# The S5 layer of a four-layer trunk: inputs regrouped through DRAM, and twelve gated outputs accumulated over K

## The chip, the cores and the metric

The kernel runs on one core of a Trainium2 chip. The metric is the device time of one execution in microseconds. "Before" is the median of three runs. The profile is one more execution, taken with the hardware profiler.

The engines are named as the profile names them. PE is TensorE, the matrix unit; PEld is its loading of weights. DVE is VectorE, ACT is ScalarE, POOL is GpSimd, and SP is SyncE, which here only issues DMAs. A matmul multiplies a weight tile (up to 128 rows by 128 columns, held in the array) with a moving tile and writes a PSUM bank. PSUM has eight banks of 128 x 512 floats here.

## The reference

The model is a trunk of four layers over one sequence of 256 tokens with 1024 channels. Layer i uses mixer i mod 3: forgetting attention (layers 0 and 3), an S5 state-space layer (layer 1), or multi-scale pooling (layer 2). A SwiGLU channel mixer (hidden width 2816) follows each. RMSNorm stands ahead of every part, and the residual is added behind it. This case is about layer 1:

```python
u = (h @ w_in).astype(F32)                                    # 256 x 1024
u_g = u.reshape(B, S, S5_GROUPS, S5_GROUP)                    # 64 groups of 16 channels
lam_bar = jnp.exp(lam * dt)                                   # 64 complex states per group
bu = jnp.einsum('gpc,bsgc->bsgp', b_bar, u_g)
_, states = lax.associative_scan(combine, (lam_seq, bu), axis=1)   # s[t] = lam_bar s[t-1] + bu[t]
y = jnp.einsum('gcp,bsgp->bsgc', c_mat, states).real.reshape(B, S, D_MODEL)
y = y + d.astype(F32) * u
g = jax.nn.gelu(y).astype(h.dtype)
val, gate = jnp.split(g @ w_glu, 2, axis=-1)
return val * jax.nn.sigmoid(gate)
```

Everything is float32. The large products are computed with the weights and the activations split into a high and a low part, three matmuls for each product.

## The kernel before

**Layout and weights.** Activations lie channel-major: eight tiles (index d, k or m) of 128 channels by 256 tokens. The weights are a list of *units* of at most 128 x 1040 floats, in the order of use (`units`, line 56). `unit` (line 102) hands out the next one. It first issues the DMA of the unit three further on (`fetch`, line 81, on SyncE's queue, four buffers `raw`), and then splits the unit two further on into high and low parts (`split_unit`, line 92: line 98 on ScalarE, line 99 on VectorE; five buffers `hl`). `term` (line 159) is the three matmuls of one 128 x 128 weight block, and `dense` (line 164) is one unit of them, 24 matmuls for one output tile. All matmuls are issued at line 157.

**Order.** A tile framework with a planner sets each engine's order of instructions. It starts from program order, simulates the engines, and lets a ready later instruction go ahead where an earlier one isn't ready; it also writes the semaphore waits, and a buffer is reused when its readers are done. On top of that the kernel has a clock of its own. `tick` (line 117) advances it after every six dense matmuls (four where two outputs are computed side by side). `at(n, fn)` files a piece of work n ticks ahead, and such a piece is queued behind the last dense matmul on TensorE. So the small work of S5 is woven into the dense work by due times.

**The S5 stage** (`s5`, line 780). The recurrence is cut into blocks of four tokens. Writing token t as 4j + r, each channel tile m needs 64 steps j of four phases r. A preparation (`prepare`, line 507), which runs during layer 0, computes for each m the tables of this scheme and stores them in DRAM (`s5d`): E, the injection weights of the four phases; tab, cosine, sine and decay per step; CX and KT, the output weights and the direct part. In the stage:

- `tables` (line 833) loads E, tab and par of tile m, on SyncE, at tick 1 + 5m. E and tab have two buffers, par three.
- The dense product with `w_s5` gives u for m = 0 and 1 side by side, then for one m after the other: 12 ticks, then four ticks for each. `evict` (line 788) scales it into u, laid out by phase as 128 channels x 4 phases x 64 steps.
- `core` (line 843), at tick 10 + 5m: for the real and the imaginary part, for each of four phases r and four groups of rows i, one matmul of E's 32 rows with u's 32 rows (line 854), accumulated over r in the PSUM tile e. It takes four banks, of which the pool `p4` holds one copy. Then VectorE rotates by cosine and sine (lines 862 to 865), scans both parts over the 64 steps of four groups (line 867), rotates back (870, 871) and writes the states sx (873, 874).
- `emit` (line 877), six ticks after the core: four full-array matmuls KT x u, 32 matmuls of 32 columns CX x sx, GELU on ScalarE (line 888), and the split into G, the eight tiles of g.
- Gating: g @ `w_glu` has eight pairs of outputs (value and gate). The first two pairs accumulate over k as G[k] appears, in two banks (lines 808 to 818). The other six pairs are dense products of their own, after all of G is there (lines 824 to 826). Each pair ends in a sigmoid, a product and the residual add (828 to 830), and `settled` (line 197) prepares the next FFN's input from it.

PSUM's eight banks are two for "acc", two for "tp" (KT and CX outputs, transposes, norms) and four that serve either as four "P" banks or as e; `open_quad` (line 150) switches between the two.

Of the kernel before, what the change touches and what calls it, by code (L numbers as in the profile page):

```python
# [16 lines left out]
D = 1024  # L17
N = 256
# [12 lines left out]
PREP_RATES = (0.08, 0.33)  # L31


class Trunk:
# [21 lines left out]
    def units(self):  # L56
# [8 lines left out]
        for l in range(self.layers):  # L65
# [6 lines left out]
            elif kind == 1:  # L72
                u.extend(a["w_s5"][m] for m in range(8))
                u.extend(a["w_glu0"][k] for k in range(4))
                u.extend(a["w_glu1"][d] for d in range(12))
            else:
                u.extend((a["w_pool"][:, 0:1024], a["w_pool"][:, 1024:2048]))
# [429 lines left out]
    def prepare(self):  # L507
# [194 lines left out]
        def gains(m):  # L702
            state["gains"] = m
            kp = self.bank("tp")
            for ri in range(2):
                for i in range(4):
                    self.mm(kp[32 * i:32 * i + 32, 0:128], XS[:, ri, 3, i], cxv[:, 0:4, i, ri], ri == 0, ri == 1)
# [6 lines left out]
        def inject(m, ri):  # L714
            pe = pp.tile([128, 4, 128], F32, tag="pe", name="pe", bufs=2)
            tp = self.bank("tp").rearrange("p (t s) -> p t s", t=4)
            for i in range(4):
                nc.tensor.transpose(tp[:, i], XS[:, ri, i].rearrange("p g c -> p (g c)"), self.ident)
# [5 lines left out]
        for m in range(8):  # L724
# [14 lines left out]
            for ri in range(2):  # L739
                for g in range(2):  # L740
                    r, c = slice(64 * g, 64 * g + 64), slice(16 * g, 16 * g + 16)
                    nc.scalar.copy(XS[r, ri, 0:3, :, c], xc[r, ri].rearrange("p (t i c) -> p t i c", t=3, i=4))
                    nc.scalar.copy(XS[r, ri, 3, :, c], bb[r, ri, qs])
# [36 lines left out]
    def s5(self, l):  # L780
# [7 lines left out]
        def evict(m, P):  # L788
            u = mp.tile([128, 4, 64], F32, tag="u", name="u", bufs=4)
            v = lambda z: z.rearrange("p (j r) -> p r j", r=4)  # L790
            nc.vector.tensor_tensor(out=u, in0=v(P), in1=v(self.R), op=ALU.mult)
            self.at(max(1, 10 + 5 * m - self.now + t0), lambda: self.core(m, u, G))

        t0 = self.now
        for m in range(8):
            self.at(1 + 5 * m, lambda m=m: self.tables(m))
        for m in range(0, 8, 2):
            P = [self.bank("acc" if m else "P")[:, 0:N] for _ in range(2)]
            if m == 0:
                self.dense(P, X)  # L800
                self.open_quad()
# [31 lines left out]
    def tables(self, m):  # L833
# [3 lines left out]
        tab = mp.tile([128, 3, 256], F32, tag="tab", name="tab", bufs=2)  # L837
        nc.sync.dma_start(tab.rearrange("p a b -> p (a b)"), self.s5d[m][:, 1024:1792])
# [4 lines left out]
    def core(self, m, u, G):  # L843
# [176 lines left out]
```

## Time and profile before

| | |
|---|---|
| Median of three runs | 1147.97 us (1147.48 to 1149.78) |
| The profiled execution's own time | 1147.19 us |
| Its span, first to last instruction | 1145.4 us |
| TensorE busy | 1117.1 us, 98% of the span |
| VectorE busy | 869.5 us, 76% |
| ScalarE busy | 681.6 us, 60% |
| Mean granted TensorE clock | 0.994 |
| Bytes moved by DMA | 224.98 MB, 196 GB/s on average |
| S5 stage, about | 335 to 444 us |

The rows quoted below come from several views. The *timeline* lists instructions in order of time, merging neighbours of one kind: start, length, engine, line, operation, output <- inputs, shapes, xcount, and in brackets the idle time before them and what ended it. *Groups by form* list line, engine, operation, shapes and count, then total busy us, mean ns of one, and idle time before them. *Stretches* give each engine's busy time within a window. *Waits* list who waited for whom: total us, times, longest. *DMA issues* list output <- input, queue, count, KB of each, and median us from issue to landing. Matmuls are pipelined and their recorded lengths overlap, so the distance between two starts says more than a length. An f32 matmul shows as two records, one of the split products as one.

### The profile page before, as it was taken

What the parts mean: (1) busy time and instruction counts of PE and PEld (TensorE: products, weight loads), DVE (VectorE), ACT (ScalarE), POOL (GpSimd) and SP (SyncE); (2) the same over time, 40 slices, a digit from 0 to 9 for tenths busy, and PEclk for the clock granted to TensorE, in tenths of its full rate; (3) what the DMA queues carried; (4) which work ended last, traced back from release to release, by engine and by line L of the source; (5) the groups of instructions that cost most, each with busy time, mean ns of one, the idle gap of its engine ahead of it and who ended that gap; (6) DMA issues with size and microseconds to landing.
All of it is one profiled execution on the core that took longest, in us unless ns stands there. A gap on an engine that the chain in (4) does not pass through costs nothing. (4 is left out here: it accounts for less than half of the span.)

```text
span 1145.4 us, 22385 instructions
## 1 busy us (share of the span) xinstructions
PE 1117.1 (98%) x8706; PEld 1026.8 (90%) x8706; DVE 869.5 (76%) x1647; ACT 681.6 (60%) x1273; POOL 132.0 (12%) x167
## 2 busy tenths in 40 slices
PE   6999999999999999999999899999999999999996
PEld 6988999999999999888888888888899899888886
DVE  6999976888959975988756688876656767988663
ACT  6467665777763254766554676665545776666551
POOL 1188000111110000000000000000004720000000
PEclk9999999999999999999999899999999999999998
DMA  8655375787888744755666255566666544755661
GB/s 270 222 182 175 122 238 189 245 264 216 264 321 324 275 140 150 234 189 188 181 177 191 93 186 194 191 178 186 196 196 218 162 140 149 214 188 189 181 188 49
DMA packets 63210, 224.98 MB, mean 196 GB/s; under 512 B 7648, under 2 KB 7984, under 8 KB 62976
## 3 DMA queue, kind: packets, MB, share of 16 engines
q1 hardware_dynamic: 56368, 200.86, 54.7%
q0 software_dynamic: 6160, 22.00, 5.8%
q8 instruction: 68, 1.11, 0.4%
q10 hardware_dynamic: 576, 0.69, 0.2%
q14 instruction: 38, 0.31, 0.1%
HBM read 208.81 MB, written 14.71 MB: 195 GB/s over the span
## 5 line engine op out<-in xcount | busy, mean ns | idle before, releaser
L157 PE MATMUL P<-X,hl 128*128 128x256 f32 (+1 forms) x4560 | 678.7, 308 | 1.3 <-ACT y L503 1.3
L157 PEld LDWEIGHTS P<-X,hl 128*128 128x128 f32 x4560 | 616.3, 189 | 52.1 <-issue 8.9
L99 DVE TENSOR_TENSOR hl<-raw,hl 128x1024 fp32r<-128x1024 f32 (+3 forms) x363 | 435.8, 1202 | 137.3 <-ACT hl L98 129.6
L98 ACT CAST hl<-raw 128x1024 fp32r<-128x1024 f32 (+3 forms) x363 | 372.1, 1028 | 174.1 <-PE acc L157 72.6
L157 PE MATMUL acc<-H,hl 128*128 128x512 f32 (+1 forms) x1628 | 251.7, 315 | 0.0
L157 PEld LDWEIGHTS acc<-H,hl 128*128 128x128 f32 x1628 | 226.8, 188 | 21.1 <-issue 0.8
L183 ACT COPY lo<-P 128x256 f32<-128x256 f32 x126 | 46.7, 371 | 102.9 <-PE P L157 102.7
L184 DVE TENSOR_TENSOR t<-P,lo 128x256 f32<-128x256 f32 x126 | 53.3, 424 | 44.6 <-ACT lo L183 44.6
L411 POOL TENSOR_SCALAR nb<-nb,c 128x128 f32<-128x128 f32 (+1 forms) x64 | 67.2, 1063 | 1.1
L157 PE MATMUL acc<-X,hl 128*128 128x256 f32 (+1 forms) x384 | 61.3, 301 | 0.2
L244 POOL TENSOR_TENSOR rs<-rs,mhalf 128x2 f32<-128x2 f32 x9 | 6.5, 719 | 474.8 <-DVE rs L243 474.8
L157 PEld LDWEIGHTS acc<-X,hl 128*128 128x128 f32 x384 | 50.6, 189 | 3.9 <-DVE X L210 0.4
L432 ACT ACTIVATE pt<-pt,st 128x128 f32<-128x128 f32 (+1 forms) x64 | 28.5, 447 | 21.7 <-DVE st L430 21.3
L157 PE MATMUL P<-hl,X 128*128 128x336 f32 (+1 forms) x192 | 41.1, 333 | 0.0
L279 ACT ACTIVATE t<-t 128x256 f32<-128x256 f32 x88 | 36.8, 418 | 6.7 <-DVE t L278 3.7
L209 ACT ACTIVATE X<-x,gains 128x256 fp32r<-128x256 f32 x55 | 27.7, 505 | 15.7 <-DVE x L264 14.9
L218 ACT ACTIVATE s<-x 128x256 f32<-128x256 f32 x63 | 25.6, 406 | 15.9 <-DVE x L264 13.1
L157 PEld LDWEIGHTS P<-hl,X 128*128 128x128 f32 x192 | 33.7, 199 | 0.0
L157 PE MATMUL acc<-hl,X 128*128 128x352 f32 x96 | 25.1, 345 | 8.7 <-DVE X L207 7.5
L210 DVE SCALAR_TENSOR_TENSOR X<-x,gains,X 128x256 fp32r<-128x256 f32 x56 | 26.9, 481 | 5.5 <-ACT X L209 5.5
L278 DVE TENSOR_TENSOR t<-t,R 128x256 f32<-128x256 f32 x66 | 28.0, 424 | 1.8
L281 DVE TENSOR_TENSOR t<-t 128x256 f32<-128x256 f32 x66 | 28.0, 424 | 1.7
(179 smaller groups left out, 855.3 us busy)
## 6 DMA issues: line engine op xcount, KB each, us to landing
raw<-in_w_gu SPq DMA_DIRECT2D x176, 512.0 KB, 3.4
raw<-in_w_dn SPq DMA_DIRECT2D x64, 512.0 KB, 3.6
raw<-in_w_qk SPq DMA_DIRECT2D x32, 512.0 KB, 4.0
raw<-in_w_dn SPq DMA_DIRECT2D x32, 384.0 KB, 3.2
raw<-in_w_fo SPq DMA_DIRECT2D x16, 512.0 KB, 3.6
raw<-in_w_glu SPq DMA_DIRECT2D x16, 512.0 KB, 4.9
raw<-in_w_vf SPq DMA_DIRECT2D x15, 520.0 KB, 4.6
nb<-nd POOLq DMA_DIRECT2D x24, 256.0 KB, 5.6
```

What stands on the lines that cost most here:

```text
L98: nc.scalar.copy(hl[:, 0, s], raw[:, s])
L99: nc.vector.tensor_tensor(out=hl[:, 1, s], in0=raw[:, s], in1=hl[:, 0, s].bitcast(F32), op=ALU.subtract)
L157: return self.nc.tensor.matmul(out, lhsT=lhsT, rhs=rhs, start=start, stop=stop).ins
L183: nc.scalar.copy(lo, o[:, N:])
L184: nc.vector.tensor_tensor(out=t, in0=o[:, 0:N], in1=lo, op=ALU.add)
L209: nc.scalar.activation(self.X[:, d, 0], x, AF.Identity, scale=g)
L210: nc.vector.scalar_tensor_tensor(out=self.X[:, d, 1], in0=x, scalar=g, in1=self.X[:, d, 0].bitcast(F32), op0=ALU.mult, op1=ALU.subtract)
L278: nc.vector.tensor_tensor(out=t, in0=t if wide else G, in1=R, op=ALU.mult)
L279: nc.scalar.activation(t, t, AF.Silu)
L281: nc.vector.tensor_tensor(out=h, in0=h if wide else U, in1=t, op=ALU.mult)
L411: nc.gpsimd.tensor_scalar(out=nb[:, i], in0=nb[:, i], scalar1=self.c[t][:, 4 * n + i:4 * n + i + 1], scalar2=None, op0=ALU.add)
L432: nc.scalar.activation(pt, pt, AF.Exp, bias=st[:, 0:1], scale=-1.0, accum_out=st[:, 1:2])
```

## The change

1. **Injection.** E keeps its size but is ordered so that for each group of rows i its 128 rows are the four phases (4 phases x 32 channels). The preparation's XS is laid out accordingly. The core then needs one matmul of 128 rows for each i and each of the two parts, eight in all, into one "tp" bank.
2. **Regrouping u.** These matmuls want u with phase and channel together on the partitions. `evict` therefore writes u to a DRAM tile `ud` (SyncE), and five ticks later four DMAs (SyncE) read it back as `ue`: 32 partitions for each phase, runs of 64 floats. `emit` still uses u itself, so u has eight buffers instead of four.
3. **Times.** Tables are due at tick 1 + 6m, core m at 18 + 6.3m but at least ten ticks after its `evict`, and `emit` seven ticks after the core.
4. **Gating.** Six pairs (twelve outputs) accumulate over k in six banks (four "P", two "acc"), with `w_glu` regrouped into 16 units of 128 x 768, two for each k. Two pairs stay as dense products, four units of 128 x 1024. The bank switch `open_quad` is no longer called here.
5. **Signed sine.** ScalarE writes a negated copy of the sine row into a fourth row of tab. The pairs of an add and a subtract (864 and 865, 873 and 874) become one 512-wide add each, with the parts read in reversed order.

```diff
             elif kind == 1:
                 u.extend(a["w_s5"][m] for m in range(8))
-                u.extend(a["w_glu0"][k] for k in range(4))
-                u.extend(a["w_glu1"][d] for d in range(12))
+                u.extend(a["w_glu0"][k] for k in range(16))
+                u.extend(a["w_glu1"][d] for d in range(4))
...
-                nc.tensor.transpose(tp[:, i], XS[:, ri, i].rearrange("p g c -> p (g c)"), self.ident)
+                nc.tensor.transpose(tp[:, i], XS[:, ri, i].rearrange("p t c -> p (t c)"), self.ident)
...
-                    nc.scalar.copy(XS[r, ri, 0:3, :, c], xc[r, ri].rearrange("p (t i c) -> p t i c", t=3, i=4))
-                    nc.scalar.copy(XS[r, ri, 3, :, c], bb[r, ri, qs])
+                    nc.scalar.copy(XS[r, ri, :, 0:3, c], xc[r, ri].rearrange("p (t i c) -> p i t c", t=3, i=4))
+                    nc.scalar.copy(XS[r, ri, :, 3, c], bb[r, ri, qs])
...
         def evict(m, P):
-            u = mp.tile([128, 4, 64], F32, tag="u", name="u", bufs=4)
+            u = mp.tile([128, 4, 64], F32, tag="u", name="u", bufs=8)
             v = lambda z: z.rearrange("p (j r) -> p r j", r=4)
             nc.vector.tensor_tensor(out=u, in0=v(P), in1=v(self.R), op=ALU.mult)
-            self.at(max(1, 10 + 5 * m - self.now + t0), lambda: self.core(m, u, G))
+            nc.sync.dma_start(self.ud[m], u.rearrange("p r j -> p (r j)"))
+            ue = mp.tile([128, 4, 64], F32, tag="ue", name="ue", bufs=4)
+
+            def load():
+                for r in range(4):
+                    nc.sync.dma_start(ue[32 * r:32 * r + 32],
+                                      self.ud[m].rearrange("(i c) (r j) -> r c i j", i=4, r=4)[r])
+
+            self.at(5, load)
+            self.at(max(10, FIRST_CORE + 63 * m // 10 - self.now + t0), lambda: self.core(m, u, ue, G))
...
-            self.at(1 + 5 * m, lambda m=m: self.tables(m))
+            self.at(1 + 6 * m, lambda m=m: self.tables(m))
...
-                self.open_quad()
                 evict(0, P[0])
...
-        acc = [self.bank("acc") for _ in range(2)]
+        outs = [self.bank(t) for t in ("P", "P", "P", "P", "acc", "acc")]
         for k in range(8):
             while self.emitted < k + 1:
                 self.tick()
-            if k % 2 == 0:
+            for h in range(2):
                 hl = self.unit()
-            for d in range(2):
-                for h in range(2):
-                    c = (k % 2 * 4 + 2 * d + h) * 128
-                    self.term(acc[d][:, h * N:h * N + N], hl, slice(c, c + 128), G, k, k == 0 and h == 0, k == 7 and h == 1)
-                self.tick()
-        self.open_quad()
+                for d in range(3):
+                    for s in range(2):
+                        c = (2 * d + s) * 128
+                        self.term(outs[3 * h + d][:, s * N:s * N + N], hl, slice(c, c + 128), G, k,
+                                  k == 0 and s == 0, k == 7 and s == 1)
+                    self.tick()
         for d in range(8):
-            if d < 2:
-                V, S = acc[d][:, 0:N], acc[d][:, N:2 * N]
+            if d < 6:
+                V, S = outs[d][:, 0:N], outs[d][:, N:2 * N]
             else:
-                V, S = self.bank("P")[:, 0:N], self.bank("P")[:, 0:N]
+                V, S = [self.bank("tp")[:, 0:N] for _ in range(2)] if d == 6 else [self.bank("P")[:, 0:N] for _ in range(2)]
...
-        e = self.p4.tile([128, 4, 512], F32, tag="e", name="e")
+        nc.scalar.activation(tab[:, 3], tab[:, 1], AF.Identity, scale=-1.0)
+        e = self.bank("tp").rearrange("p (a n) -> p a n", a=2)
         for ri in range(2):
-            for r in range(4):
-                for i in range(4):
-                    rows = slice(32 * i, 32 * i + 32)
-                    self.mm(e[:, i, 64 * ri:64 * ri + 64], E[rows, ri, r], u[rows, r], r == 0, r == 3)
-        two = lambda z: z.unsqueeze(1).broadcast_to([128, 2, 256])
-        c2, s2 = two(tab[:, 0]), two(tab[:, 1])
+            for i in range(4):
+                self.mm(e[:, ri, 64 * i:64 * i + 64], E[:, ri, i], ue[:, i], True, True)
+        c2 = tab[:, 0].unsqueeze(1).broadcast_to([128, 2, 256])
+        sn = tab[:, 1:4:2]
...
-        nc.vector.tensor_tensor(out=ij(A), in0=ev, in1=ij(c2), op=ALU.mult)
-        nc.vector.tensor_tensor(out=ij(B), in0=ev, in1=ij(s2), op=ALU.mult)
-        nc.vector.tensor_tensor(out=A[:, 0], in0=A[:, 0], in1=B[:, 1], op=ALU.add)
-        nc.vector.tensor_tensor(out=A[:, 1], in0=A[:, 1], in1=B[:, 0], op=ALU.subtract)
+        nc.vector.tensor_tensor(out=A, in0=e, in1=c2, op=ALU.mult)
+        nc.vector.tensor_tensor(out=B, in0=e[:, ::-1], in1=sn, op=ALU.mult)
+        nc.vector.tensor_tensor(out=A, in0=A, in1=B, op=ALU.add)
...
-        nc.vector.tensor_tensor(out=B, in0=A, in1=s2, op=ALU.mult)
-        v4 = lambda z: z.rearrange("p (i j) -> p i j", i=4)[:, :, 0:63]
-        nc.vector.tensor_tensor(out=sx[:, 0, :, 1:64], in0=v4(C[:, 0]), in1=v4(B[:, 1]), op=ALU.subtract)
-        nc.vector.tensor_tensor(out=sx[:, 1, :, 1:64], in0=v4(C[:, 1]), in1=v4(B[:, 0]), op=ALU.add)
-        self.at(6, lambda: self.emit(m, u, CX, KT, sx, G))
+        nc.vector.tensor_tensor(out=B, in0=A[:, ::-1], in1=sn[:, ::-1], op=ALU.mult)
+        v4 = lambda z: z.rearrange("p a (i j) -> p a i j", i=4)[:, :, :, 0:63]
+        nc.vector.tensor_tensor(out=sx[:, :, :, 1:64], in0=v4(C), in1=v4(B), op=ALU.add)
+        self.at(7, lambda: self.emit(m, u, CX, KT, sx, G))
```

`FIRST_CORE` is 18. `layout` reorders `w_glu` for the new units.

More of the change, by code (lines that the diff above doesn't have):

```diff
@@ L31 @@
 PREP_RATES = (0.08, 0.33)
+FIRST_CORE = 18
 class Trunk:
@@ L706, in gains @@
                 for i in range(4):
-                    self.mm(kp[32 * i:32 * i + 32, 0:128], XS[:, ri, 3, i], cxv[:, 0:4, i, ri], ri == 0, ri == 1)
+                    self.mm(kp[32 * i:32 * i + 32, 0:128], XS[:, ri, i, 3], cxv[:, 0:4, i, ri], ri == 0, ri == 1)
             for i in range(4):
@@ L836, in tables @@
         nc.sync.dma_start(E.rearrange("p a b c -> p (a b c)"), self.s5d[m][:, 0:1024])
-        tab = mp.tile([128, 3, 256], F32, tag="tab", name="tab", bufs=2)
-        nc.sync.dma_start(tab.rearrange("p a b -> p (a b)"), self.s5d[m][:, 1024:1792])
+        tab = mp.tile([128, 4, 256], F32, tag="tab", name="tab", bufs=2)
+        nc.sync.dma_start(tab[:, 0:3].rearrange("p a b -> p (a b)"), self.s5d[m][:, 1024:1792])
         par = mp.tile([128, 1536], F32, tag="par", name="par", bufs=3)
@@ L841, in tables, with core @@
         self.tabs[m] = (E, tab, par)
-    def core(self, m, u, G):
+    def core(self, m, u, ue, G):
         nc, mp = self.nc, self.mp
@@ L859, in core @@
         C = mp.tile([128, 2, 256], F32, tag="C", name="C", bufs=1)
-        ev = e[:, :, 0:128].rearrange("p i (a j) -> p a i j", a=2)
-        ij = lambda z: z.rearrange("p a (i j) -> p a i j", i=4)
-        nc.vector.tensor_tensor(out=ij(A), in0=ev, in1=ij(c2), op=ALU.mult)
-        nc.vector.tensor_tensor(out=ij(B), in0=ev, in1=ij(s2), op=ALU.mult)
-        nc.vector.tensor_tensor(out=A[:, 0], in0=A[:, 0], in1=B[:, 1], op=ALU.add)
-        nc.vector.tensor_tensor(out=A[:, 1], in0=A[:, 1], in1=B[:, 0], op=ALU.subtract)
+        nc.vector.tensor_tensor(out=A, in0=e, in1=c2, op=ALU.mult)
+        nc.vector.tensor_tensor(out=B, in0=e[:, ::-1], in1=sn, op=ALU.mult)
+        nc.vector.tensor_tensor(out=A, in0=A, in1=B, op=ALU.add)
         for ri in range(2):
@@ L915, in run @@
         self.early = {0: [piece(1, 3)], 1: [piece(3, 8)]}
+        self.ud = [self.dp.tile([128, 256], F32, name=f"ud{m}") for m in range(8)]
         self.s5d = [self.dp.tile([128, 3328], F32, name=f"s5d{m}") for m in range(8)]
@@ L986, in layout @@
     w = f["s5_w_glu"][0].reshape(D, 2, 8, 128)
-    o["w_glu0"] = w[:, :, 0:2].reshape(4, 2, 128, 2, 2, 128).transpose(0, 2, 1, 4, 3, 5).reshape(4, 128, 1024)
-    o["w_glu1"] = np.stack([tiles(w[:, h, 2:].reshape(D, 768)) for h in range(2)], 1).reshape(12, 128, 1024)
+    o["w_glu0"] = w[:, :, 0:6].reshape(8, 128, 2, 2, 3, 128).transpose(0, 3, 1, 4, 2, 5).reshape(16, 128, 768)
+    o["w_glu1"] = np.stack([tiles(w[:, h, 6:].reshape(D, 256)) for h in range(2)], 1).reshape(4, 128, 1024)
     o["w_pool"] = f["pool_w"][0].reshape(4, 2, 128, 256).transpose(2, 0, 1, 3).reshape(128, 2048)
```

## The prediction, made before the result was known

> **What bounds the kernel now.** First I read the head of the page, then the stretches of the S5 stage, then TensorE's timeline in that stage, and last its waits. "Core m" below is the work that the function `core` issues for channel tile m.
>
> ```profile
> span 1145.4 us, 22385 instructions
> PE 1117.1 (98%) x8706; PEld 1026.8 (90%) x8706; DVE 869.5 (76%) x1647; ACT 681.6 (60%) x1273; POOL 132.0 (12%) x167
> ```
> ```profile
> 343.50:400.00 56.50, 55.19 (x1143) 52.18 (x1144) 52.93 (x94) 16.56 (x22) 0.00 (x0) 1.00 0.83 302
> 400.00:410.70 10.70, 10.55 (x190) 9.67 (x189) 6.47 (x12) 4.75 (x7) 0.00 (x0) 1.00 0.31 96
> 410.70:443.80 33.10, 33.10 (x283) 33.10 (x282) 24.99 (x39) 19.68 (x33) 0.00 (x0) 1.00 0.55 175
> ```
> The stretches give start and end, length, then busy time and instructions of PE, PEld, DVE, ACT, POOL, granted clock, DMA share, GB/s. TensorE sets the pace: 55.19 of 56.50 us while the cores run, all of 33.10 us afterwards. VectorE is second and nearly full in the first stretch (52.93 of 56.50), so a change there counts only if it frees TensorE or holds it up. The edit can gain only TensorE time within the stage, and this is how one core looks there:
>
> ```profile
> 394.51 2.77 PE L157 MATMUL acc<-X,hl 128*128 128x256 f32 x22
> 397.21 2.02 PE L157 MATMUL e<-u,E 32*128 32x64 f32 x64
> 399.15 0.98 PE L157 MATMUL acc<-X,hl 128*128 128x256 f32 x6
> 399.97 1.31 PE L157 MATMUL tp<-u,par 128*128 128x256 f32 x8
> 401.21 1.10 PE L157 MATMUL tp<-sx,par 128*32 128x64 f32 x64
> 402.24 3.49 PE L157 MATMUL acc<-X,hl 128*128 128x256 f32 x24
> 405.57 1.31 PE L157 MATMUL tp<-u,par 128*128 128x256 f32 x8
> ```
> ```profile
> 409.09 1.79 PE L157 MATMUL acc<-X,hl 128*128 128x256 f32 x12
> 410.72 33.23 PE L157 MATMUL P<-X,hl 128*128 128x256 f32 x280
> 443.78 0.40 PE L157 MATMUL acc<-X,hl 128*128 128x512 f32 x1
> ```
> Since the durations overlap, I use differences of start times. A dense matmul costs (443.78 - 410.72)/280 = 0.118 us, and a tick of the schedule (six of them) 0.71. The group e took 399.15 - 397.21 = 1.94, and entering it 397.21 - 394.51 - 22 x 0.118 = 0.10 more: **2.04 us per core**. The KT group took 1.24, the sx group 402.24 - 401.21 = 1.03.
>
> **The change, part by part.**
>
> *The e matmuls.* Before: 32 matmuls per core, each of 32 rows, shown as 64 records (an f32 matmul leaves two). After: eight of 128 rows, so 16 records of 128x128 weights by 64 columns. No row shows 16 such records in sequence, so the price needs bounds. The upper one is a run of full-array f32 weight loads whose matmuls stream one column each:
>
> ```profile
> 338.38 0.52 PEld L157 LDWEIGHTS tp<-cst,sq 128*128 128x128 f32 x4 [0.26 <-DVE sq L221]
> 338.82 0.30 PEld L157 LDWEIGHTS P<-X,hl 128*128 128x128 f32 x2
> ```
> Four loads in 338.82 - 338.38 = 0.44: 0.11 us per record, though almost nothing streams; 16 x 0.11 = 1.76. The lower one assumes that the load hides and only columns count: KT streams 2 x (256+192+128+64) = 1280 columns in 1.24 us, 0.97 ns each, 64 columns 0.062, 16 records 0.99. I take 0.11: a matmul shorter than its weight load can't hide it. So the quadrupled array use buys little. The 64 old records ran as 16 fours, and 1.94/16 = 0.12 says that a four already cost about one load. What goes is the entry and exit of the 32-row mode: 2.04 - 1.76 = 0.28 per core, times eight **2.2 us** (by the lower bound 1.05 x 8 = 8.4).
>
> [...]
>
> *Instruction supply.* Two sx groups, of cores 1 and 4, stop in the middle with nothing to wait for:
>
> ```profile
> 359.14 0.69 PE L157 MATMUL tp<-sx,par 128*32 128x64 f32 x33
> 360.47 0.65 PE L157 MATMUL tp<-sx,par 128*32 128x64 f32 x31 [0.64 <-issue]
> 361.05 0.38 PE L157 MATMUL acc<-X,hl 128*128 128x256 f32 x1
> ```
> ```profile
> 384.17 0.86 PE L157 MATMUL tp<-sx,par 128*32 128x64 f32 x44
> 385.67 0.53 PE L157 MATMUL tp<-sx,par 128*32 128x64 f32 x20 [0.63 <-issue]
> 386.12 0.39 PE L157 MATMUL acc<-X,hl 128*128 128x256 f32 x1
> ```
> ```profile
> q8 instruction: 9, 0.15, 1.0%
> ```
> They last 1.91 and 1.95 us where 1.03 is usual: 1.8 us lost. In 343.5 to 400 the instruction queue moved nine blocks while TensorE ran 1143 + 1144 instructions, 254 per block. My reading is that TensorE ran out of instructions where blocks are used up fastest: a core with its 5 ticks of dense work is 64+8+64+30 = 166 records, 332 instructions, in 1.94+0.10+1.24+1.03+3.55 = 7.9 us, or 6.0 us a block. After: 16+8+64+38 = 126 records in 1.76+1.24+1.03+4.5 = 8.5 us, 8.6 us a block. I credit **1.5** of the 1.8, because cores 0 and 1 start two ticks apart and may still crowd a block. The bounds are 0 and 1.8.
>
> [...]
>
> *The gating matmuls and the end of the cores.* Twelve outputs instead of four accumulate over k; their 384 dense matmuls stay. Before, 52 ticks carry the dense work up to k=7 while the last `emit` is due at tick 51, and TensorE shows it: the 24 records from 402.24 took 3.33 instead of 2.83, the 12 from 409.09 took 1.63 instead of 1.42. After, `emit` 7 is due at tick 62+7 = 69 and k=7 begins at 36+6x7 = 78. **0.7 us** goes. The bounds are 0 and 0.9.
>
> *The round trip of u.* The first matmul of core 0 waits for four loads of a DRAM tile that SyncE has just written.
>
> ```profile
> 342.34 1.15 DVE L791 TENSOR_TENSOR u<-P,R 128x256 f32<-128x256 f32 x2 [3.16 <-PE P L157]
> 343.54 2.01 PE L157 MATMUL e<-u,E 32*128 32x64 f32 x64 [0.25 <-DVE u L791]
> ```
> ```profile
> nd<-nct SPq DMA_DIRECT2D x2, 16.0 KB, 3.2
> ```
> ```profile
> E<-s5d SPq DMA_DIRECT2D x6, 512.0 KB, 6.0
> ```
> ```profile
> L840 SPq DMA_DIRECT2D par<-s5d x8: 319/335/512, 337.0 to 386.2; - x8
> ...
> DMA to landing us min/median/max: 4.7/7.1/8.9
> ```
> Today's wait for u (**0.25 us**) goes. The u of tile 0 is ready at 342.34 + 1.15/2 = 342.9. Its write lands 3.2 to 6.0 later, 346.1 to 348.9; four issues at 0.335 add 1.3, and the loads land at 350.6 to 356.2. Core 0 is due ten ticks after 342.3, at 349.4. It is late by 1.2 to 6.8 us if TensorE's order is fixed by the ticks; it isn't, since other ready dense work can be planned ahead of it, and that bounds the wait by 0. I take **1.3 us** of new wait. Core 1, two ticks later behind core 0's 1.76, has its data one set of issues (1.3) after core 0; from core 2 on there are 14 ticks or more and other cores between, so I price them at nothing. Without that cover each costs what core 0 does.
>
> *SyncE's queue.* Behind the write (which waits for VectorE's u) and the loads (which wait for the write) stand weight fetches and table loads.
>
> ```profile
> SPq L87 <- DVE hl L99: 57.6, 19, 6.9
> ```
> Between 330 and 450 us SyncE itself stands 57.6 us waiting for free weight buffers, so five more issues per tile (40 x 0.335 = 13 us) fit. If fetches fell late, VectorE's and ScalarE's casts and then TensorE would wait; the cover is three units of 24 matmuls (8.5 us) against 6.0 to land. The 2.1 MB that u adds are an eighth of the 17 MB (302 GB/s x 56.5 us) that this stretch moves.
>
> *VectorE and ScalarE.*
>
> ```profile
> L870 DVE TENSOR_TENSOR C<-A,tab 128x512 f32<-128x512 f32 x8 | 5.5, 690 | 0.2
> ```
> ```profile
> L864 DVE TENSOR_TENSOR A<-A,B 128x256 f32<-128x256 f32 x8 | 3.4, 424 | 0.2
> ```
> ```profile
> L99 DVE TENSOR_TENSOR hl<-raw,hl 128x1024 fp32r<-128x1024 f32 x314 | 385.4, 1229 | 110.4 <-ACT hl L98 103.2
> L99 DVE TENSOR_TENSOR hl<-raw,hl 128x768 fp32r<-128x768 f32 x32 | 30.6, 957 | 12.1 <-ACT hl L98 11.6
> ```
> Two pairs of 256-wide adds become two of 512: 2 x (0.85 - 0.69) x 8 = 2.6 us less for VectorE. The weight subtractions, 16 x 0.957 + 4 x 1.229 instead of 16 x 1.229, cost 0.6 more. ScalarE negates the sine rows, eight short operations beside 16.56 busy of 56.50 us; the casts stand behind them if a table lands late. TensorE gets nothing from either, because VectorE stays below it. At the end six outputs want VectorE at once: in 410.7 to 443.8 it spent 24.99 us, less 12 casts 10.2, 1.7 per output for six. Six of them plus four casts are 15.1 us against 96 dense matmuls (11.3): up to 3.8 us of backlog. I price it at nothing, because the forgetting-attention layer ends with eight outputs at once and its FFN lost at most this:
>
> ```profile
> PE acc L157 <- DVE X L210: 1.2, 1, 1.2
> ```
> The new layout of XS in the preparation keeps the number of copies and transposes: nothing.
>
> **Sum.** The profiled execution took 1147.19 us for a span of 1145.4. 2.2 + 1.5 + 0.7 + 0.25 = 4.65 off, 1.3 on: -3.35, so 1143.8. The profiled execution stands 0.8 below the median of the three runs (1147.97); at the level of that median this is **1144.6 us**. The measurement can tell about 0.2%, or 2.3 us, from no change.
>
> **The rivals.** *Given back:* the data of core 0 arrives 4 to 5 us late, or the backlog of 3.8 us at the end is paid; -4.65 + 4.5 is no change, 1147.8. For it: the landing rows. Against: the planner may fill the gap. *Only columns count:* with 0.062 per record another 6.2 go, 1138.4. For it: KT's pace. Against: the 0.11 row. *Slower:* both trips of tile 0 take the longest landing seen, 8.9. The loads land at 342.9 + 8.9 + 1.3 + 8.9 = 362.0, core 0 waits 12.6, and the time is 1147.97 - 4.65 + 12.6 = 1155.9. It is slower once the wait exceeds 4.65 + 2.3 = 7.0 us, data after 356.4. For it: the DMA share of 0.83 over the cores' stretch. Against: 8.9 is the longest of eight loads six times as large.
>
> **How the numbers follow.** Forecast 0.52 (its own range 1143.0 to 1146.6: fetch gain 0 to 1.8, wait 0 to 3), given back 0.27, only columns 0.07, slower 0.14. Range 1141.0 to 1150.5: it drops most of the slow case and the columns case, which together hold 0.2. Faster by over 0.2% (below 1145.7): four fifths of the forecast and the columns case, with a little of the second, 0.50; same 0.36; slower 0.14.
>
> **What would show it.** Right: 16 records of e per core starting about 0.11 us apart, a core's e near 1.8 us; no sx group of 1.9 us with an idle row put down to issue; dense rows at 0.118 up to k=7. Wrong: e near 1.0 us per core; TensorE idle before e, released by the DMA of ue, for more than 3 us; idle rows before the first FFN matmuls of layer 1 behind X, or casts waiting for weight DMAs in the cores' stretch.

## The result, and the profile after

The changed kernel takes **1182.59 us** (median of 4 runs, 1181.67 to 1183.07) beside 1148.88 for the kernel before (median of 4, 1147.48 to 1150.28): a ratio of 1.0302, with a 95% interval of 1.0286 to 1.0318. The forecast was 1144.6 and the range ended at 1150.5, so both were wrong.

The head of the page after, and three rows of TensorE's timeline after that mark the S5 stage (start, duration, engine, line, operation, tiles, count):

```profile
span 1180.4 us, 21680 instructions
PE 1129.3 (96%) x8322; PEld 1038.2 (88%) x8322; DVE 869.3 (74%) x1635; ACT 685.1 (58%) x1285; POOL 133.6 (11%) x167
```
```profile
337.89 3.28 PE L158 MATMUL P<-X,hl 128*128 128x256 f32 x26
...
476.31 0.51 PE L158 MATMUL acc<-X,hl 128*128 128x512 f32 x2
...
603.01 3.23 PE L158 MATMUL acc<-H,hl 128*128 128x512 f32 x17
```
TensorE has fewer matmul records (8322 instead of 8706) and is still busy 12 us longer. The stage runs from the first dense matmul of its input projection to the first matmul of layer 1's FFN: 476.31 - 337.89 = 138.42 us. Before, the same two points stood at 335.04 and 443.78, so it took 108.74. Of the 35.0 us by which the span grew, **29.7** lie in this stage. Another 2.85 lie ahead of the stage and 3.0 at the head of the FFN behind it (see the last two experiments); what follows takes 0.5 less. For the experiments I use the longer stretch up to the FFN's second half, where all kernels are alike again: 265.12 us after, and before

```profile
567.47 9.84 PE L157 MATMUL acc<-H,hl 128*128 128x512 f32 x55
```
567.47 - 335.04 = 232.43. What lies ahead of the stage is left out of the comparison, since it varies by itself: two kernels below with the same work there reach the stage at 335.06 (no_trip) and at 337.21 (no_trip_gate2).

Inside the stage, TensorE waits. Its waits after, from 335 to 480 us (what was waited for, total, times, longest):

```profile
PE P L158 <- ACT hl L99: 13.2, 2, 8.5
PE tp L158 <- DMA ud<-u: 7.5, 1, 7.5
PE tp L158 <- DVE sx L878: 1.1, 1, 1.1
```
That is 21.8 us. The stretches of the stage after (PE, PEld, DVE, ACT, POOL busy, then granted clock, DMA share, GB/s) show a second loss:

```profile
335.00:360.00 25.00, 24.46 (x205) 24.06 (x203) 11.69 (x18) 9.39 (x15) 1.42 (x4) 1.00 0.69 248
360.00:385.00 25.00, 16.41 (x216) 15.63 (x215) 15.73 (x26) 2.69 (x6) 0.00 (x0) 0.73 0.61 178
385.00:412.00 27.00, 18.52 (x221) 17.36 (x221) 13.31 (x21) 5.39 (x10) 0.00 (x0) 0.75 0.59 185
412.00:430.00 18.00, 13.30 (x124) 12.58 (x128) 7.35 (x11) 4.71 (x7) 0.00 (x0) 0.72 0.68 213
430.00:476.00 46.00, 46.00 (x565) 45.27 (x555) 37.78 (x60) 25.74 (x42) 0.00 (x0) 1.00 0.62 212
```
The granted clock is 0.73, 0.75 and 0.72 in the three stretches with the waits, and 1.00 in the first and the last. TensorE's timeline after shows what that means:

```profile
345.27 15.04 PE L158 MATMUL acc<-X,hl 128*128 128x256 f32 x125
360.15 1.89 PE L158 MATMUL tp<-ue,E 128*128 128x64 f32 x16
...
376.97 3.65 PE L158 MATMUL tp<-ue,E 128*128 128x64 f32 x16 [7.52 <-DMA ud<-u]
...
384.75 1.56 PE L158 MATMUL P<-X,hl 128*128 128x256 f32 x11
...
401.91 2.43 PE L158 MATMUL P<-X,hl 128*128 128x256 f32 x8 [8.48 <-ACT hl L99]
...
411.79 2.25 PE L158 MATMUL P<-X,hl 128*128 128x256 f32 x16
...
420.15 2.43 PE L158 MATMUL P<-X,hl 128*128 128x256 f32 x8 [4.70 <-ACT hl L99]
...
429.18 1.10 PE L158 MATMUL tp<-sx,par 128*32 128x64 f32 x64
...
442.86 1.89 PE L158 MATMUL tp<-ue,E 128*128 128x64 f32 x16
...
445.89 1.10 PE L158 MATMUL tp<-sx,par 128*32 128x64 f32 x64
446.92 1.69 PE L158 MATMUL P<-X,hl 128*128 128x256 f32 x12
```
Here `tp<-ue,E` is a core's e group, `tp<-u,par` its KT group and `tp<-sx,par` its sx group. Undisturbed, the three take 446.92 - 442.86 = 4.06 us. Right after the first long wait they take 384.75 - 376.97 = 7.78. After the second, those three and the eight dense matmuls ahead of them take 411.79 - 401.91 = 9.88 instead of 4.06 + 8 x 0.118 = 5.0. Behind the third, thirteen dense matmuls, e and KT take 429.18 - 420.15 = 9.03 instead of 4.6. The granted clock in these three (376.97 to 384.75, 401.91 to 411.79 and 420.15 to 429.18) was 0.50, 0.50 and 0.51, beside 1.00 from 442.86 to 446.92. So each stall is paid again behind it: 3.7 + 4.9 + 4.4 = **13.0 us at half clock on top of 21.8 us of waiting**. Together that is 34.8 us. Less the 5.6 that the change gains where nothing waits (the first experiment), it is 29.2, of 29.7 measured.

What is late can be read from SyncE's own timeline after (its DMA issues, in the order in which they stand in its queue), and from its waits:

```profile
352.50 4.53 SPq L798 DMA_DIRECT2D ue<-ud  x8
362.07 0.34 SPq L845 DMA_DIRECT2D E<-s5d  x1
362.51 0.38 SPq L793 DMA_DIRECT2D ud<-u  x1
362.94 0.42 SPq L798 DMA_DIRECT2D ue<-ud  x1
366.11 0.32 SPq L845 DMA_DIRECT2D E<-s5d  x1
367.17 0.32 SPq L847 DMA_DIRECT2D tab<-s5d  x1
367.54 0.90 SPq L798 DMA_DIRECT2D ue<-ud  x2
369.51 0.34 SPq L849 DMA_DIRECT2D par<-s5d  x1
372.51 0.34 SPq L847 DMA_DIRECT2D tab<-s5d  x1
372.90 0.42 SPq L798 DMA_DIRECT2D ue<-ud  x1
...
393.73 0.34 SPq L847 DMA_DIRECT2D tab<-s5d  x1
...
395.06 0.42 SPq L88 DMA_DIRECT2D raw<-in_w_glu  x1
```
```profile
SPq L845 <- PE tp L158: 25.2, 5, 6.6
SPq L847 <- DVE B L876: 12.8, 6, 4.7
SPq L849 <- PE tp L158: 10.2, 4, 3.5
```
By the order of the queue, the four loads of the u of core 2 are issued at 362.94, twice from 367.54 on, and at 372.90. Loads of ue land 3.8 us after their issue in the median, so the last of them lands at about 376.7, and core 2 starts at 376.97. (The wait's row names a write, ud; but these matmuls read ue, and I take the load for what they waited for.) Between the four stand the loads of later table tiles, and each of these waits for a buffer: E (line 845) until the e group of an earlier core has read it, tab (847) until VectorE has used it, par (849) until TensorE has. So SyncE stands, the loads of u behind it stand, core 2 waits for them, and the next table buffer comes free only when a core has run. The fetches of the gating weights stand in the same queue. The one issued at 395.06 stood behind the table load of 393.73, and ScalarE's cast waits for it, in its timeline:

```profile
401.03 0.83 ACT L99 CAST hl<-raw 128x768 fp32r<-128x768 f32 x1 [3.38 <-DMA raw<-in_w_glu]
```
That is what TensorE's matmuls at 401.91 wait for; those at 420.15 wait in the same way for a fetch issued at 415.10, behind a table load of 414.72. Meanwhile the DMA engines are partly idle: their busy share is 0.61, 0.59 and 0.68 in the three stretches with the waits (178, 185 and 213 GB/s), against 0.83 (302 GB/s) in the cores' stretch before.

### The profile page after: what moved, and what is told of

It is laid out like the page before. It is cut to its first block, busy times and chain, and to the rows that moved or that the text cites. A ratio compares the mean times of both kernels' runs of the same rounds, so it can differ in the third digit from the quotient of the medians.

```text
span 1180.4 us, 21680 instructions
## 1 busy us (share of the span) xinstructions
PE 1129.3 (96%) x8322; PEld 1038.2 (88%) x8322; DVE 869.3 (74%) x1635; ACT 685.1 (58%) x1285; POOL 133.6 (11%) x167
## 5 line engine op out<-in xcount | busy, mean ns | idle before, releaser
L158 PE MATMUL P<-X,hl 128*128 128x256 f32 (+1 forms) x4512 | 681.2, 309 | 14.6 <-ACT hl L99 13.2
L892 ACT ACTIVATE g<-tp 128x256 f32<-128x256 f32 x8 | 5.1, 632 | 47.0 <-PE tp L158 47.0
```

The costliest lines, as they stand in the source:

```text
L158: return self.nc.tensor.matmul(out, lhsT=lhsT, rhs=rhs, start=start, stop=stop).ins
```

## The experiments

Three theories for the loss, with the letters of the first four expectations: L, the trip of u through DRAM is too long by itself; Q, the trip, the table loads and the weight fetches hold each other up in SyncE's one queue; B, the table loads do it alone, because they are due before their buffers are free. All runs stand beside runs of the kernel before on the same chip. "Stretch" is the time from the stage's first matmul to the FFN's second half in the profiled run, less the 232.43 us of before. In the last column, hl are split weights, ue the regrouped u, sx the states, B the product that the rotation reads from e, g the output of GELU, X split activations (G among them), and sq the squares for the FFN's norm.

| kernel | median us (runs) | ratio to before, 95% interval | stretch, us | main waits of TensorE in it, us |
|---|---|---|---|---|
| after | 1182.59 (4) | 1.0302 [1.0286, 1.0318] | +32.7 | hl 13.2, ue 7.5 (row ud) |
| no_trip | 1145.90 (5) | 0.9992 [0.9967, 1.0017] | -2.3 | sq 1.2 |
| trip_pool | 1154.93 (3) | 1.0053 [1.0030, 1.0075] | +6.3 | ue 3.0, sq 1.7 |
| tables_pool | 1156.31 (3) | 1.0058 [1.0036, 1.0081] | +7.5 | sq 3.6, ue 2.5 |
| tables_late | 1166.83 (2) | 1.0151 [1.0122, 1.0181] | +16.1 | hl 6.2, sx 2.7 |
| tables_bufs4 | 1162.44 (2) | 1.0129 [1.0094, 1.0164] | +11.1 | hl 4.4, sx 2.9 |
| before_full | 1145.27 (10) | 0.9978 [0.9966, 0.9990] | -3.3 | u 0.2 |
| trip_pool_gap | 1150.02 (10) | 1.0019 [0.9998, 1.0040] | -0.9 | ue 2.4, sq 1.1 |
| trip_direct | 1165.53 (2) | 1.0157 [1.0122, 1.0193] | +13.2 | ue 6.3, X 2.4 |
| no_trip_gate2 | 1148.57 (10) | 1.0007 [0.9995, 1.0018] | +0.2 | X 2.3 |
| regroup_pool | 1149.68 (10) | 1.0012 [0.9993, 1.0030] | +3.6 | ue 1.8, sq 1.7 |
| regroup_act | 1156.65 (4) | 1.0079 [1.0058, 1.0099] | +6.5 | B 2.3, g 1.7, sx 1.2 |
| regroup_first | 1146.67 (12) | 0.9990 [0.9979, 1.0002] | -3.6 | sq 1.5 |
| regroup_eight | 1155.13 (6) | 1.0058 [1.0044, 1.0072] | +7.3 | sx 5.0 |
| regroup_eight_b | 1149.14 (12) | 1.0006 [0.9991, 1.0022] | -1.2 | X 1.2, hl 0.8 |

**no_trip: the change without the trip.** The full-array matmuls read `u` itself; the regrouping is left out.

```
-            nc.sync.dma_start(self.ud[m], ...); ue = mp.tile(...); four loads, due five ticks later
+            ue = u
```


> The changed kernel without the trip through DRAM: the full-array matmuls read u itself, whose rows aren't regrouped, so the injection computes something else; everything else (tables, due times, gating, queues for the rest) is that of the changed kernel. Theory Q (SyncE's one queue: what waits in it for a buffer, for u or for the written copy holds up all that stands behind) leaves the table loads ahead of the weight fetches, so a part of the 20.7 us of TensorE waits stays: 1150 to 1165 us. Theory L (the two dependent DMAs of the trip are simply too long) expects all new waits gone: 1143 to 1147 us. Theory B (tables are due before their buffers are free) expects little: 1170 to 1180 us.

1145.90 us: L's number, and below the range of Q. All of the loss comes with the trip, and none with the rest of the change. Q expected that the table loads alone would go on holding up the weight fetches. SyncE does still wait 36.0 us for table buffers here (12.9, 14.3 and 8.8 for E, tab and par), but TensorE waits for no weights, so that part of Q is refuted. TensorE's timeline of no_trip around the first core:

```profile
342.45 7.26 PE L158 MATMUL acc<-X,hl 128*128 128x256 f32 x60
349.55 1.90 PE L158 MATMUL tp<-u,E 128*128 128x64 f32 x16
351.25 1.68 PE L158 MATMUL acc<-X,hl 128*128 128x256 f32 x12
```
The e group takes 1.70 us, and the first core follows 60 dense matmuls, not 125. So in the kernel after most of the projection's matmuls stand ahead of core 0, which hid the trip there and left the later cores uncovered. My reading is that the planner moved them there because it counts the trip; no run tests that, and in trip_pool, with the same trip on another queue, it put only 69 there. The stage takes 103.18 us, 5.56 less than before. No_trip does not yet say whether the trip's length or its place in the queue costs the time.

**trip_pool, tables_pool: two queues instead of one.** In trip_pool the write and the four loads of u go to GpSimd's queue; in tables_pool u stays and the three table loads go there.

```
-            nc.sync.dma_start(self.ud[m], ...)       # and the four loads of ue
+            nc.gpsimd.dma_start(self.ud[m], ...)     # trip_pool
-        nc.sync.dma_start(E..., self.s5d[m][:, 0:1024])        # and tab, par
+        nc.gpsimd.dma_start(E..., self.s5d[m][:, 0:1024])      # tables_pool
```


> The changed kernel with the write of u and the four loads of ue issued from GpSimd's queue, everything else the same. Theory Q: the table and weight DMAs no longer stand behind the trip, nor the trip behind the tables; most of the loss is given back, 1143 to 1152 us. Theory L: the trip takes as long as before, 1175 to 1185 us. Theory B: table loads that wait for buffers still hold up the weights on SyncE, 1165 to 1180 us.

> The changed kernel with the three table loads of each tile issued from GpSimd's queue; the trip of u and the weights stay on SyncE. Theory Q: the weights and the trip stand behind no buffer wait any more, but still behind the write of u and its landing: 1145 to 1160 us. Theory L: 1175 to 1185 us. Theory B: the early due times do no harm when nothing stands behind them, 1143 to 1150 us.

1154.93 and 1156.31. Q gave up to 1152 and up to 1160, so trip_pool lies 3 us above its range; L and B miss both runs by 6 us or more. Either separation gives back 25 to 26 of the 32.7 us of the stretch. The trip itself is hardly shorter: write and load land in 4.7 and 3.6 us in trip_pool (medians from issue), against 4.5 and 3.8 in the kernel after. And in trip_pool SyncE waits for table buffers as long as in the kernel after, 48.9 us against 48.2:

```profile
SPq L845 <- PE tp L158: 26.2, 6, 16.2
SPq L849 <- PE tp L158: 11.7, 5, 3.0
SPq L847 <- DVE B L876: 11.0, 5, 3.4
```
These waits cost little once the loads of u don't stand behind them. So it is neither the trip nor the table waits alone, but their sharing a queue. One thing moves along: the order of TensorE, with fewer dense matmuls ahead of core 0; tables_bufs4 below separates that. TensorE's longest wait in trip_pool from 335 to 470 us, and the stretch behind it:

```profile
PE tp L158 <- DMA ue<-ud: 3.0, 1, 3.0
```
```profile
355.00:362.00 7.00, 6.36 (x30) 6.39 (x31) 2.64 (x5) 0.00 (x0) 4.47 (x10) 0.52 0.45 98
```
What the trip itself costs is this: write issued at 345.2, first e matmul at 355.6, a wait of 3.0 us for core 0 alone, and 7 us at a granted clock of 0.52 behind it, worth some 3.4.

**tables_late: tables due one tick behind the core that frees their buffer.**

```
-            self.at(1 + 6 * m, lambda m=m: self.tables(m))
+            self.at(1 + 6 * m if m < 2 else max(22, FIRST_CORE + 63 * (m - 2) // 10) + 1, ...)
```


> The changed kernel with the tables of tile m, from m = 2 on, due one tick after core m-2, which is where they stood before; everything else is the same. Theory B: the waits for table buffers vanish from SyncE's queue and the time falls to 1143 to 1152 us. Theory Q in the form that the trip itself blocks the queue: 1165 to 1185 us. Theory L: 1175 to 1185 us.

1166.83: half of the loss comes back. That is the lower end of Q's range and 15 us above B's. TensorE still waits for casts (hl 6.2 us), and the due times of the tables alone are not the cause.

**tables_bufs4: same queue, four buffers for each table tile.**

```
-        E = mp.tile([128, 2, 4, 128], F32, tag="E", name="E", bufs=2)     # tab 2, par 3
+        E = mp.tile([128, 2, 4, 128], F32, tag="E", name="E", bufs=4)     # tab 4, par 4
```


> The changed kernel with four buffers instead of two and three for the three table tiles; u's writes and loads stay on SyncE's queue with all else. No table load waits for a free buffer any more, so nothing on SyncE stands behind such a wait; but the order of TensorE has all 144 dense matmuls of the input projection ahead of the first core. Theory Q (what costs is that the loads of u and the weight fetches stand behind table loads that wait for buffers): most of the loss goes, 1152 to 1162. Rival C (what costs is that the cores have no dense work left beside them, whatever SyncE does): 1172 to 1185. Rival L (the DMA engines are full, the trips are long on any queue): 1170 to 1185, with ue landing later than 6 us after its issue.

1162.44, 0.4 us above Q's range: 21.6 of the 32.7 us come back with every DMA still on SyncE's queue. SyncE's waits for E, tab and par buffers fall from 48.2 us (the three rows of after) to 5.3. The DMA issues from 330 to 450 us (KB each, median us from issue to landing):

```profile
ud<-u SPq DMA_DIRECT2D x8, 128.0 KB, 6.2
ue<-ud SPq DMA_DIRECT2D x32, 32.0 KB, 4.9
```
In the kernel after they landed in 4.5 and 3.8 us. So here both legs of the trip are *longer* and the kernel is 20 us faster: neither the length of a trip nor full DMA engines explain the loss; the waits in the queue explain two thirds of it. All 144 dense matmuls of the projection still stand ahead of core 0, so the order of TensorE can't be what gave these two thirds back. What is left fits rival C, and how much of it is C's was not separated. In its timeline TensorE runs

```profile
343.98 17.28 PE L158 MATMUL acc<-X,hl 128*128 128x256 f32 x144
361.10 3.68 PE L158 MATMUL tp<-ue,E 128*128 128x64 f32 x32
```
the 144 dense matmuls and then two e groups with nothing beside them, and later waits 2.9 for sx and 4.4 for hl.

**before_full: the form of the matmuls alone.** The kernel before with eight full-array matmuls on `u` as it stands, so the injection computes something else.

```
-            for r in range(4):
-                for i in range(4): ... self.mm(e[...], E[rows, ri, r], u[rows, r], r == 0, r == 3)
+            for i in range(4):
+                self.mm(e[:, i, 64 * ri:64 * ri + 64], E[:, ri, i], u[:, i], True, True)
```


> The kernel before with one edit: the 32 injection matmuls of 32 rows of each core become the eight full-array matmuls of the change, reading u as it stands (not regrouped, so this part of the computation is another one). No u goes through DRAM, four outputs accumulate over k as before, the sine rows and the order of the rest are as before. Theory F (the form of the matmuls alone pays, as the prediction priced it): 2.2 us off for the entry and exit of the 32-row mode and 1.5 for the instruction supply, so 3.7 below the kernel before, about 1144.5 to 1145.5, with no sx group of 1.9 us. Rival G (the 5.7 us that the stage lost in no_trip came from the twelve gated outputs and the order, and the form gives nothing): within 1 us of the kernel before, 1147.5 to 1149.

1145.27, ratio 0.9978 with an interval below 1: theory F. The stage is 3.3 us shorter (3.7 were expected), and no idle time of TensorE in it is put down to issue any more (1.3 us in two sx groups before). The part of the change that was meant to pay does pay, about 2.5 us or 0.22%.

**trip_pool_gap and trip_direct: can the trip be hidden or halved?** In the first, core 0 is due fifteen ticks after its u instead of ten. In the second, sixteen copies of 32 x 64 per tile go from `u` to `ue` without DRAM, on GpSimd's queue.

```
+FIRST_CORE = 23;  max(15, ...)                                              # trip_pool_gap
+                nc.gpsimd.dma_start(ue[32*r:32*r+32, i], u[32*i:32*i+32, r])   # trip_direct, 16 per tile
```


> As trip_pool (writes and loads of u on GpSimd's queue), but core 0 is due fifteen ticks after its u instead of ten, and the other cores move with it. Theory T (what trip_pool still pays in the stage is the latency of tile 0's trip, a wait of 3.0 us, and the half-clock stretch behind it, 3.4): 1154.9 less 6.4, so 1147.5 to 1150. Rival E (moving the cores later only moves the cost to the end of the stage, where the six outputs wait for VectorE): the wait for ue goes, but idle time of 3 us or more stands before the FFN of layer 1, and it is 1153 to 1157.

> As trip_pool, but u does not go through DRAM: sixteen copies of 32 x 64 from u to ue on GpSimd's queue for each tile, one trip instead of two. Theory W (latency of the two trips is what trip_pool still pays): the data of core 0 comes 3 to 5 us sooner, no wait for ue, about 1148 to 1151. Rival I (issues: sixteen of 0.55 us are 8.8 us a tile against 2.8 in trip_pool, 70 us for eight tiles, more than the 60 us in which the cores run): ue late for several cores, 1160 to 1175.

trip_pool_gap: 1150.02, at the top end of theory T, but not for T's reason. The wait for ue stays (2.4 us), since the trip took longer: from the issue of the write to the first e matmul 359.1 - 346.7 = 12.4 us, 10.4 in trip_pool. The half-clock stretch behind it is absent in the profile (granted clock 1.00 from 359.1 to 366.0 us); the ten times reach from 1145.68 us, at a mean granted clock of 0.995, to 1156.17, at 0.987, so it may come and go. trip_direct: 1165.53, in rival I's range. The issues take 0.50 us each, and beside that GpSimd's queue waits 17.4 us, in 19 places, for earlier copies to land, which I had not named; TensorE waits four times for ue.

**no_trip_gate2: the old gating.** no_trip with four accumulated outputs instead of twelve.

```
-        outs = [self.bank(t) for t in ("P", "P", "P", "P", "acc", "acc")]
+        acc = [self.bank("acc") for _ in range(2)]          # and the loops of the kernel before
```


> As no_trip (the full-array matmuls read u itself, which leaves the regrouping out), but with the gating of the kernel before: four gated outputs accumulate over k, twelve follow in full. Theory O (twelve accumulated outputs cost a backlog on VectorE at the end of the stage: a wait of 1.2 us and a half-clock stretch worth 1.7 behind it, less the 0.7 us that the fuller gating gave): about 2 below no_trip, 1143 to 1144.5. Rival P (the twelve outputs pay for themselves through the cover they give the cores): 1146 to 1149, with idle TensorE between the cores.

1148.57: rival P. The wait for sq goes, as O said, but TensorE now waits five times among the cores for X, here the G of the core just done (2.3 us): the gating matmul that needs it comes too soon behind the core.

**regroup_pool, regroup_act, regroup_first: regrouping on the chip.** Sixteen copies of 32 x 64 per tile, to other partitions, on GpSimd, on ScalarE, or on GpSimd with half of tiles 0 and 1 on ScalarE. No write, no load.

```
-            nc.sync.dma_start(self.ud[m], ...)   # and the loads
+                        nc.gpsimd.tensor_copy(out=ue[32*r:32*r+32, i], in_=u[32*i:32*i+32, r])   # regroup_pool
+                        nc.scalar.copy(ue[32*r:32*r+32, i], u[32*i:32*i+32, r])                  # regroup_act
+                        (nc.scalar.copy if m < 2 and i % 2 else nc.gpsimd.tensor_copy)(...)      # regroup_first
```


> The change with the regrouping done on the chip instead of through DRAM: sixteen copies of 32 x 64 on GpSimd for each tile move u's blocks to other partitions; no write, no load, no wait on SyncE. Theory R (the form of the matmuls pays and all of the loss is the trip): the stage as in no_trip, about 103 us, 1144 to 1147, some 2 to 3 below the kernel before. Rival S (GpSimd's copies are the new trip): nothing shows their price; between its memset of 0.11 us and its smallest tensor_scalar of 0.89 us sixteen are 1.8 to 14 us a tile; above 0.4 us each they are slower than a core every 6.3 ticks, TensorE waits before e, and it is 1152 to 1165.

> The same with the sixteen copies on ScalarE. ScalarE's copy of 64 x 64 took 0.244 us, so 3.9 us a tile and 31 for eight, beside 16.6 busy in the 56.5 us of the cores. Theory R: it fits, 1144 to 1149. Rival S (the copies stand in front of the weight casts and of the gelu on ScalarE, so that hl or g comes late): idle TensorE of 3 us or more put down to ScalarE, half-clock stretches behind it, 1152 to 1160.

> As regroup_pool, but of the first two tiles, whose copies come at once, half go to ScalarE: 6.6 us of copies for both instead of 13.2 on GpSimd alone. Theory R (what regroup_pool still paid at the cores was the wait of 1.8 us of core 1 and the half-clock stretch of 3.4 us behind it, worth 1.7): 1149.7 less 3.5, so 1145 to 1147.5, below the kernel before. Rival D (the kernel before and this one differ by the end of the stage: six outputs at once on VectorE, a wait of 1.2 to 1.7 us and a half-clock stretch in the FFN behind it): the wait for ue goes, the time stays within 1.5 us of the kernel before.

regroup_pool: 1149.68, between the two theories. From its waits and its tile ue:

```profile
PE tp L158 <- POOL ue L798: 1.8, 1, 1.8
```
```profile
L798 POOL COPY ue<-u x128: 226/233/1161, 344.8 to 402.5; 32x64 f32<-32x64 f32 x128
```
Only core 1 waits, because tiles 0 and 1 come at once. regroup_act: 1156.65, in rival S's range: the copies are short (31.0 us for 128), but the gelu (g), sx and VectorE's reading of e come late. Only 1.7 us of the waits are put down to ScalarE itself, less than the 3 that S named. regroup_first: **1146.67**, in R's range; but it lies 1.1 us below the kernel before, which rival D (within 1.5) allowed too, and the wait that D named at the end of the stage is there (sq 1.5). The wait for ue is gone and the stage takes 439.39 - 336.22 = 103.17 us, as in no_trip. It is 36 us faster than the kernel after. Against the kernel before its interval, 0.9979 to 1.0002, still holds no change, so it is not shown to beat it.

**regroup_eight, regroup_eight_b: where the rest of the gain goes.** The stage of regroup_first is 5.6 us shorter than before, but up to the FFN's second half only 3.6 are left. The head of the FFN in regroup_first, and the same 69 matmul records before:

```profile
439.40:453.40 14.00, 11.94 (x69) 9.80 (x68) 6.56 (x17) 4.59 (x11) 1.86 (x3) 1.00 0.36 116
```
```profile
443.78:455.78 12.00, 11.56 (x69) 9.77 (x67) 3.14 (x7) 2.61 (x6) 1.83 (x3) 1.00 0.43 137
```
The columns are those of the stretches above. It takes two us more, with VectorE twice as busy (6.56 against 3.14): it still works on the last outputs, and the FFN's statistics wait 1.5 us for it. The two kernels that follow accumulate eight outputs instead of twelve.

```
-        outs = [self.bank(t) for t in ("P", "P", "P", "P", "acc", "acc")]
+        outs = [self.bank("P") for _ in range(4)]      # w_glu0 in 8 units of 1024
-FIRST_CORE + 63 * m // 10
+FIRST_CORE + 6 * m                                     # regroup_eight: and FIRST_CORE = 14
```


> As regroup_first, but eight gated outputs accumulate over k instead of twelve, the other eight follow in full, and the cores are due four ticks sooner and six ticks apart. Theory O (the part of the loss that is left once the trip is gone is the end of the stage, where six finished pairs want VectorE at once: a wait of 1.5 us before the statistics of the FFN and at times a half-clock stretch behind it): that wait falls below 0.5 us and the time is 1.5 to 3 below regroup_first, 1143.5 to 1145.5. Rival C (with fewer gated matmuls the cores lose their cover): idle TensorE of 2 us or more between 355 and 425 us, 1147 to 1153.

> The question of regroup_eight again, with the cores due from tick 18 on as in regroup_first, six ticks apart, so that core 2 comes after the last matmuls of core 0 again (in regroup_eight its scan overwrote the state that they read, so that part of its computation was another one). Eight gated outputs accumulate over k, eight follow in full. Theory O (the end of the stage, six finished pairs at once on VectorE, takes what the trip's removal gave): the wait before the FFN's statistics falls from 1.5 below 0.5 us, 1.5 to 3 below regroup_first, 1143.5 to 1145.5. Rival C (cover lost): idle TensorE of 2 us or more between 355 and 435 us, 1147 to 1153. Rival N (the end is not it): the wait goes and the time stays at 1146 to 1147.5.

regroup_eight (1155.13) says nothing on the question: core 2 came ahead of the end of core 0, whose last matmuls waited 5.0 us. regroup_eight_b (1149.14) took the wait for sq away, as O said, but 2.0 us of waits for X and hl came up among the cores: rival C. Twelve outputs cost about 2 us at the end, fewer cost as much in the middle. Neither is free: at four, eight and twelve outputs some of what was gained in the stage is lost again.

## Why the prediction was wrong, step by step

*The e matmuls* (2.04 to 1.76 us a core) held: 1.70 measured in no_trip, 0.106 us a record against 0.11, so 2.7 us for eight cores where 2.2 were priced. The rival that only columns count (0.99 a core) is refuted.

*Instruction supply* (1.5) held in its effect: in before_full and no_trip no wait of TensorE in the stage is put down to issue, and a whole sx group takes 1.03 us there. That blocks used up too fast were the reason was not tested. With the first step 3.7 were priced; before_full's stage is 3.3 shorter and its time 2.5.

*The gating and the end of the cores* (0.7): the stage of no_trip is 2.2 us shorter than that of before_full, more than was priced. But the *end of six outputs*, which was priced at nothing with a bound of 3.8, costs 2.0 in regroup_first, and 3.2 in no_trip, where eight dense matmuls behind the waits, from 449.87 to 452.43 us, also started 0.32 us apart, beside 0.175 for the 28 from 439.99 to 444.88 ahead of them. Both lie within the bound, and the value taken was wrong: the comparison with the forgetting-attention layer did not carry over, and why not stays open.

*The round trip of u* (1.3 for core 0, bound 6.8) lay within its bound for a trip on a queue without table waits, at about twice the value: 3.0 in trip_pool, 2.4 in trip_pool_gap. In the kernel after core 0 doesn't wait at all, since dense work stands ahead of it; that this work is then missing beside the later cores was not seen. The sentence that **fails is "from core 2 on there are 14 ticks or more and other cores between, so I price them at nothing"**: core 2 waited 7.5 us.

*SyncE's queue* is **the step that failed**. The prediction read SyncE's 57.6 us of waiting as room: five more issues of 0.335 us "fit". But SyncE's queue worked in order (its rows from 362 to 373 us: the issues of the four loads of core 2 stretch from 362.94 to 372.90 us), and such a queue has no room behind an instruction that waits. Three kinds of work now stand in it whose waits depend on each other: table loads wait for a core to free a buffer, the loads of u behind them feed that core, and the weight fetches behind both feed the matmuls that cover it. The prediction even listed what stands behind the write and the loads, but not what stands *ahead* of them, the loads of E and tab with two buffers each. The profile before had this to read: beside the 57.6 us for weight buffers its table loads waited 28.9 us from 330 to 450 us, among them

```profile
SPq L838 <- DVE B L871: 10.1, 3, 4.1
```
for a tab buffer (line 838) that VectorE still used. Two separations gave back about four fifths of the loss in the stretch, and more buffers on the same queue two thirds. Two of the prediction's own signs of being wrong came: TensorE idle ahead of e for more than 3 us, and casts waiting for weight DMAs.

*The slower rival* had the right object and the wrong mechanism: one long trip, paid once (1155.9). That a wait comes back for several cores, and that each is paid again at half clock (13.0 of 34.8 us), was in no case. The range lacked the price of a wait, which was only the wait itself.

## What to carry to other kernels

Idle time of an in-order queue is not capacity (here 57.6 us of SyncE's): before adding a transfer, write down the order of its issues and ask of each what it waits for, and whether what stands behind it feeds that very thing. A dependent transfer belongs on a queue on which nothing waits for its own consumer, or the waiting loads need enough buffers (here 25 to 26 and 21.6 of 32.7 us came back). And where the trace shows the granted clock falling behind a TensorE stall of a few us, price the stall at about twice its length: here 1.8 us cost 1.7 more (regroup_pool), 3.0 cost 3.4 (trip_pool) and 4.7 cost 4.4 (after), but 7.5 only 3.7 and 8.5 only 4.9 (after), and 2.4 nothing (trip_pool_gap).

## What was not expected of the hardware

The granted clock fell to one half behind a single wait of 1.8 us in regroup_pool: it was 0.50 from 359.40 to 362.80 us. Behind one of 2.4 us in trip_pool_gap it was 1.00 from 359.10 to 366.00. The stretches behind the two waits, columns as above:

```profile
359.40:362.80 3.40, 3.40 (x18) 3.40 (x17) 2.33 (x4) 0.00 (x0) 3.03 (x9) 0.50 0.77 245
```
```profile
359.10:366.00 6.90, 6.88 (x60) 6.90 (x61) 4.88 (x8) 0.83 (x1) 5.87 (x11) 1.00 0.71 190
```
So here a wait of 2.4 us cost its length in one run, and one of 1.8 us nearly twice that in another (1.8 and half of the 3.4 us at 0.50), which may be part of why the times of one kernel spread over 5 to 10 us; that was not tested.

GpSimd's copies of 32 x 64 to other partitions took 0.233 us in the median, but up to 1.16 (mean 0.41 over 128, regroup_pool); ScalarE's took 0.242 in the mean over 128 (regroup_act). What ran beside the long ones was not tested.
